# Block writes on SyncE's queue, an earlier split of the receptance, and a second bank for key turns, in a two-layer decoder trunk

## Chip, cores and metric

One core of one Trainium2 chip. The metric is the device time of one launch in microseconds, the median over several runs. Three runs of the kernel before are given, and one execution was taken with the hardware profiler.

## What is computed

Two residual layers over a sequence of 512 tokens of width 2048, all in float32: `x <- x + W_out(mixer(RMSNorm(x)) * silu(gate))`. The first mixer is a gated differential attention with 8 heads (two softmaxes per head on query and key halves of 128, values of 256). The second is a gated RWKV-7 time mixing with 32 heads of width 64. Its core is a scan over tokens:

```python
def step(S, inp):
    r_t, w_t, k_t, v_t, a_t, b_t = inp
    sa = jnp.einsum('bhvk,bhk->bhv', S, a_t)
    S = S * w_t[:, :, None, :] + sa[..., None] * b_t[:, :, None, :] + v_t[..., None] * k_t[:, :, None, :]
    y = jnp.einsum('bhvk,bhk->bhv', S, r_t)
    return S, y
```

with `a = -kk` and `b = kk * a_iclr`, where `kk` is a normalised key. The receptance `r`, key `k`, value `v` and gate are columns of `h @ w_in`, each mixed with its own value one token earlier.

## The kernel before

**Numbers.** Each float32 operand of a large product is split into a rounded part and a rest (`wh` by ScalarE at L105, `wl` by VectorE at L106), and three matmuls take the place of one (`mm3`). So the product of one 128 x 128 weight block with 512 tokens is three matmuls, and TensorE's time is above all in those (L122, L566).

**Order of the work.** Side work (attention of the head before, the scan of the pair before) is cut into steps by Python generators. A `Chain` holds one; `tick` (L169) is called after every matmul of the large products and lets the chain go one step when so many matmuls have passed as the last `yield` said. The framework then orders each engine's instructions; `high_priority(offset=...)` moves an instruction forward by that offset (`AHEAD` 2000, `SCAN` 3000, `SOLVE` 4000), and `issue_after` keeps it behind a given one. Each engine runs its own list in order and waits on semaphores of the others. DMAs are started from the lists of SyncE, ScalarE and GpSimd, each with its own queue.

**First layer** (`layer0`, up to about 955 us). For each head: a product for queries and keys, one for values and gate, and beside them the attention of the head before. `turn_qk` (L291) transposes one of four blocks of 128 tokens of a head's queries and keys on TensorE into a PSUM bank `pt` of tag "pb" (L295), copies it to `qkT` (ScalarE, L298) and subtracts to get the rest `qkL` (VectorE, L299). The tag "pb" has one bank in this pool, shared with the turns of the attention weights (`turn`, L363) and of the result (`turn_y`, L391); the tag "pc" has one, used by `weigh`. For heads 1 to 7 the key blocks 0 and 1 are turned by a chain of their own, and 2 and 3 (the list `rest`) within the attention steps. For head 0 all four are turned by one chain, which `finish` empties after the product of values and gate. At the end of the layer `half_h` and `more_h` transpose the new x and `make_h` (L1088, L1089) scales and splits it into `hH` and `hL` for the second layer's first products (`lora`).

**Second layer** (`layer1`). Two heads make a pair; 16 pairs follow one another, each with four products (k, r, v, gate) of 48 matmuls. For each pair j:

- `stage2` (L1271, L1272) makes `AR`, the scaled receptance and query, and `rf` from the mixed receptance (`mixr`).
- `gram` runs inside the product for v: 16 matmuls `gp` (L1287), copies into `G` (ScalarE, L1294), a sum of squares for the key norms (`ssl`, L1299), and six writes of blocks of G and of the norms to `ltd` in HBM (L1301, L1307).
- `t_solve` loads the blocks from `ltd` into `LT`, spread over 128 partitions (GpSimd's queue, L1341), and inverts unit lower triangular blocks of 32 by 32 on VectorE in 31 steps of two instructions (L1352, L1354), from L1343 to L1355. The result `Tm` is written to `td` (GpSimd's queue, L1356).
- `t_combine`, one pair later, loads `td` into `TT` (SyncE's queue, L1369), transposes on VectorE (`T`, L1378), and makes the off-diagonal blocks with matmuls `px` (L1384, L1394).
- `scan_pair` then goes through 8 chunks: `sm` from VS and G (L1465), copy to `rhs`, `sm` from rhs and TT (L1476), copy to VS, `sm` from VS and BKT (L1483), and VectorE's L1487 (L1490 for the first chunk), which makes the state VS of the next chunk. GpSimd keeps the states (`SA`, L1471) and scales them (`Sg`, L1474), which L1487 reads. GpSimd also masks G (L1316, L1318).
- `stage_v` sums r k over channels (L1206, L1207, on the split `sHx`, `sLx` of `rf`, L1097, L1098), mixes v and makes `y` (L1408). `group_norm` (L1531 to L1537) and `finish_y` work on pair j - 2.

Of the kernel before, what the change touches and what calls it, by code (L numbers as in the profile page):

```python
# [13 lines left out]
F32 = mybir.dt.float32  # L14
# [9 lines left out]
P = 128  # L24
# [263 lines left out]
            w.tile([P, 4, T], F32R, name="qkL", tag="qkL", bufs=1))  # L288


def turn_qk(g, t1s, qkT, qkL, t):  # L291
    nc = g.nc
    pt = g.ps.tile([P, 512], F32, name="pt", tag="pb")
    for c in range(4):
        nc.tensor.transpose(pt[:, c * P : (c + 1) * P], t1s[t][:, c * P : (c + 1) * P], g.ident[:])  # L295
    ts = slice(t * P, (t + 1) * P)
    pv = pt[:].rearrange("p (c q) -> p c q", c=4)
    nc.scalar.copy(qkT[:, :, ts], pv)  # L298
    nc.vector.tensor_sub(qkL[:, :, ts], pv, qkT[:, :, ts].bitcast(F32))  # L299
# [26 lines left out]
def attention(g, h, qkT, qkL, sq, V, VL, G, gap, rows=None, keys=()):  # L326
# [87 lines left out]
    for i in range(NT + 3):  # L414
        if i > 1 and i < NT + 2:
            weigh(i - 2)
        if i > 2:
            turn_y(i - 3)
        if i < NT + 2:
            yield 10  # L420
        while due:
            store(*due.pop())
        if i == NT + 2:
            break
        if 0 < i <= NT:
            turn(i - 1)
        if i < NT:
            scores(i)
        if i == 0 and keys:
            yield 7  # L430
            turn_qk(*keys[0])
            yield 9
            turn_qk(*keys[1])
            yield max(gap - 26, 6)
        else:
            yield gap - 10
    if rows is not None:
        rows += last

# [353 lines left out]
def layer0(g, aps):  # L793
# [3 lines left out]
    with ExitStack() as cx:  # L797
# [91 lines left out]
        for h in range(NH):  # L889
            if h:  # L890
                Chain(g, attention(g, h - 1, *before, 26, keys=rest), 56 if h > 1 else 20)
            t1s = [t1_tile() for _ in range(NT)] if h else t1s
            sq = g.small.tile([P, NT, 2], F32, name="sq", tag="sq")
            qkT = head_qkT(g)

            def keys(n, t1s=t1s, qkT=qkT):
                for t in range(n):
                    turn_qk(g, t1s, *qkT, t)
                    if t < n - 1:
                        yield 20  # L900

            rest = [(g, t1s, *qkT, t) for t in (2, 3)] if h else ()
            if h:
                values = unit_head(g, aps, h, t1s, sq, lambda: Chain(g, keys(2), 6))
            else:
                for ts in ([0, 1], [2, 3]):
                    head_qk(g, t1s, sq, ts)
                Chain(g, keys(NT), 120)
                input_sums(g, pairs, False)
                ps = unit_tok(g, g.hH, g.hL, vg_cols(aps, h), 512)  # L910
                acc1 = g.work.tile([P, 2, 512], F32, name="acc1", tag="acc1", bufs=1)
                G, vg = gates(g)
                vg += [acc1[:, 0], acc1[:, 1]]
                copy_out(g, vg, ps)
                for c in list(g.chains):
                    c.finish(g)
                input_sums(g, pairs, True)
                first_tiles(g, aps, 1)
                values = head_vg(g, h, vg, G)
            before = qkT + (sq,) + values  # L920
            if h == 0:
                Chain(g, rwkv_consts(g, aps))
                g.chains[0].step(g)
# [93 lines left out]
        def half_h(k, half, m, bank=(g.ps, "pa", 2)):  # L1017

            ps = bank[0].tile([P, 512], F32, name="xT", tag=bank[1], bufs=bank[2])
            for i in range(2):  # L1020
                xq, c0 = xs[(k + i) // 4], (k + i) % 4 * P
                for t in range(2):
                    tt, at = 2 * half + t, (2 * i + t) * P
                    if c0 == 0 and half:
                        scale((k + i) // 4, tt)
                    with tc.issue_after(m.ins) if m else ExitStack():
                        nc.tensor.transpose(ps[:, at : at + P], xq[:, tt, c0 : c0 + P], g.ident[:])
            for i in range(2):
                with tc.high_priority(offset=AHEAD):
                    make_h(g, ps[:, 256 * i : 256 * i + 256], KT + k + i, k + i, half)  # L1030

        def begin(m):
# [170 lines left out]
def sum_channels(g, out, ones, x):  # L1203

    h, l = x
    g.nc.tensor.matmul(out, ones, h[:], start=True, stop=False)  # L1206
    g.nc.tensor.matmul(out, ones, l[:], start=False, stop=True)  # L1207
# [68 lines left out]
def gram(g, j, p, before):  # L1276

    nc, w, BK = g.nc, g.work, p.BK
    p.G = w.tile([P, NC_, 2, 2, C], F32, name="G1", tag="G1", bufs=2)
    p.BKT = w.tile([P, NC_, P], F32, name="BKT", tag="BKT", bufs=2)  # L1280
    halves = []
    for c0, tag in ((0, "pb"), (4, "pc")):
        gp = [g.ps.tile([P, 512], F32, name="gp", tag=tag, bufs=2) for _ in range(2)]
        halves.append((c0, gp))
        for i in range(4):
            for h, r_ in ((0, slice(0, C)), (1, slice(C, P))):
                m = nc.tensor.matmul(gp[h][:, i * P : (i + 1) * P], BK[r_, c0 + i, :, :], p.AR[r_, c0 + i, :, :],  # L1287
                                     start=True, stop=True)
    if before:
        with g.tc.issue_after(m.ins):  # L1290
            before.step(g)
    for c0, gp in halves:
        for h in range(2):
            nc.scalar.copy(p.G[:, c0 : c0 + 4, :, h, :], gp[h][:].rearrange("p (u x t) -> p u x t", u=4, x=2))  # L1294
    ps = g.ps.tile([P, 512], F32, name="pt", tag="pb", bufs=2)
    sum_channels(g, ps[:2, :], g.ones[:, 0 : P : C], p.k2)
    ss = w.tile([2, T], F32, name="ssl", tag="thg", bufs=1)
    with g.tc.high_priority(offset=SOLVE if j == D // P - 1 else 0):
        nc.scalar.copy(ss[:], ps[:2, :])  # L1299
        for half in range(2):  # L1300
            nc.scalar.dma_start(  # L1301
                out=g.ltd[j % 2, half, :, :, HALF, :],
                in_=ss[:].rearrange("h (c b t) -> h c b t", c=NC_, b=2)[:, :, half, :])
        for half in range(2):
            for h in range(2):
                q0 = h * C + half * HALF
                nc.scalar.dma_start(  # L1307
                    out=g.ltd[j % 2, half, h, :, 0:HALF].rearrange("c s t -> s c t"),
                    in_=p.G[q0 : q0 + HALF, :, 0, h, half * HALF : (half + 1) * HALF])

# [90 lines left out]
def stage_v(g, j, p, vps):  # L1401
    nc, w = g.nc, g.work
    col = lambda n: g.prm[n][:, j : j + 1]
    ps = g.ps.tile([P, 512], F32, name="pt", tag="pd", bufs=1)
    sum_channels(g, ps[:], g.ones[:], split_act(g, p.rf[:], w, "x"))
    v = shift_mix(g, vps, P, *mus(g, 2, j), "v", 1)
    p.y = w.tile([P, T], F32, name="y", tag="y", bufs=4)
    nc.vector.tensor_mul(p.y[:], ps[:], v[:])  # L1408
# [140 lines left out]
def layer1(g, aps):  # L1549
    nc, tc = g.nc, g.tc  # L1550
    with ExitStack() as cx:
# [22 lines left out]
        for j in range(D // P):  # L1574
# [13 lines left out]
            def behind(m, j=j, p=p):  # L1588
                if j > 1:
                    pairs[j - 2].chain.finish(g)  # L1590
                with tc.issue_after(m.ins):
                    gram(g, j, p, j > 2 and pairs[j - 1].chain)
                if j == 2:
                    pairs[1].chain.wait = 16
                mask_gram(g, p, 0)
# [159 lines left out]
```

## Time and profile before

| what | value |
|---|---|
| median of 3 runs | 2150.44 us (2147.19 to 2150.76) |
| the profiled execution, its own time | 2153.95 us |
| its span in the profile | 2152.2 us |
| TensorE (PE) busy | 2104.0 us, 98% |
| VectorE (DVE) busy | 1613.1 us, 75% |
| ScalarE (ACT) busy | 1153.1 us, 54% |
| GpSimd (POOL) busy | 386.0 us, 18% |
| mean granted clock of TensorE | 0.988 |

The profile shows one execution. An engine's busy time counts its instructions; idle time ahead of an instruction is put down to the instruction whose semaphore came last. In the rows `out<-in` are the program's names of the tiles, `L1384` is a line of the kernel before, and `[0.57 <-DVE T L1378]` says that the engine was idle for 0.57 us until VectorE's T of line 1378 was done. The granted clock is TensorE's share of its full clock. A "frame" in what follows is a pair's own time, counted along with TensorE's matmuls.

### The profile page before, as it was taken

How to read it: one execution, taken by the hardware profiler on the slowest of the kernel's cores; microseconds unless marked ns; L12 is line 12 of the kernel's file. 1: busy time of each engine (PE TensorE's matmuls, PEld its weight loads, DVE VectorE, ACT ScalarE, POOL GpSimd, SP SyncE). 2: the span in 40 equal slices, each digit the busy share in tenths (PEclk: the TensorE clock that was granted, in tenths of full speed). 3: DMA queues.
4: the chain of work that ended last, by engine and by line, in shares of the span. 5: the costliest groups of instructions: out<-in, count | busy, mean ns of one | idle time of the engine just before them, and what ended most of it. 6: DMA issues, size and time to landing. Idle time of an engine off the chain costs nothing.

```text
span 2152.2 us, 34019 instructions
## 1 busy us (share of the span) xinstructions
PE 2104.0 (98%) x11852; PEld 1706.3 (79%) x11852; DVE 1613.1 (75%) x4129; ACT 1153.1 (54%) x2278; POOL 386.0 (18%) x751
## 2 busy tenths in 40 slices
PE   9999999999999999999899999999999999999999
PEld 7788888888887788878677787888888888878887
DVE  6888888888888885667677578777777787767645
ACT  5666556565565543355454455555555556645322
POOL 1011211202113000101322212222222222221001
PEclk9999999999999999999899999999999999999999
DMA  8487978879789836623222223223333233346555
GB/s 264 128 180 188 174 170 187 161 187 175 170 184 221 295 118 186 140 80 104 68 79 68 84 79 94 84 83 94 100 88 92 83 97 91 104 127 191 178 162 120
DMA packets 143101, 294.60 MB, mean 137 GB/s; under 512 B 47968, under 2 KB 65376, under 8 KB 142928
## 3 DMA queue, kind: packets, MB, share of 16 engines
q1 hardware_dynamic: 75072, 178.55, 26.4%
q0 software_dynamic: 25216, 87.74, 22.5%
q10 hardware_dynamic: 42640, 26.14, 4.0%
q8 instruction: 93, 1.52, 0.3%
q14 instruction: 80, 0.66, 0.1%
HBM read 268.71 MB, written 23.66 MB: 136 GB/s over the span
## 4 chain that ended last, share of the span: by engine, by line
PE 36%; DVE 9%; DMA 3%; issue 2%; ACT 1%; POOL 0%; ACTq 0%; SPq 0%; DVEq 0%; POOLq 0%
PE pp L122 22%; PE pt L122 5%; DMA td<-Tm 2%; DVE tmpl L1352 2%; DVE wl L106 2%; DVE Tm L1354 1%; PE gp L1287 1%; PE sm L1465 1%; DMA TT<-td 1%; PE sm L1476 1%; PE sm L1483 1%; PE px L1384 1%; PE px L1394 1%; DVE VS L1487 1%; PE pt L1207 0%
## 5 line engine op out<-in xcount | busy, mean ns | idle before, releaser
L106 DVE TENSOR_TENSOR wl<-wraw,wh 128x1024 fp32r<-128x1024 f32 (+2 forms) x291 | 356.1, 1224 | 222.6 <-ACT wh L105 210.7
L105 ACT CAST wh<-wraw 128x1024 fp32r<-128x1024 f32 (+2 forms) x291 | 304.4, 1046 | 339.3 <-PE pp L122 175.0
L122 PE MATMUL pp<-hH,wl 128*128 128x512 f32 x1024 | 417.0, 407 | 0.0
L122 PE MATMUL pp<-hL,wh 128*128 128x512 f32 x1024 | 415.7, 406 | 0.0
L122 PE MATMUL pp<-hH,wh 128*128 128x512 f32 x1024 | 413.3, 404 | 0.0
L122 PEld LDWEIGHTS pp<-hH,wh 128*128 128x128 f32 x1024 | 195.0, 190 | 35.9 <-issue 1.5
L122 PEld LDWEIGHTS pp<-hL,wh 128*128 128x128 f32 x1024 | 195.0, 190 | 35.6 <-issue 0.3
L122 PEld LDWEIGHTS pp<-hH,wl 128*128 128x128 f32 x1024 | 195.0, 190 | 33.2 <-DVE wl L106 0.5
L566 PE MATMUL pp<-wh,hH 128*128 128x512 f32 x448 | 178.1, 397 | 0.0
L566 PE MATMUL pp<-wh,hL 128*128 128x512 f32 x448 | 176.5, 394 | 0.0
L122 PE MATMUL pp<-wh,hH 128*128 128x512 f32 x372 | 145.8, 392 | 1.7 <-ACT hH L1088 1.6
L122 PE MATMUL pp<-wl,hH 128*128 128x512 f32 x372 | 146.0, 393 | 0.4 <-DVE wl L106 0.4
L122 PE MATMUL pp<-wh,hL 128*128 128x512 f32 x372 | 145.8, 392 | 0.1
L1352 DVE SCALAR_TENSOR_TENSOR tmpl<-LT,Tm 128x60 f32<-128x60 f32 (+24 forms) x496 | 135.0, 272 | 11.6
L1471 POOL COPY SA<-VS 64x64 f32<-64x64 f32 x224 | 63.0, 281 | 442.8 <-DVE VS L1487 348.0
L566 PE MATMUL pp<-wl,hH 128*128 128x512 f32 x448 | 140.6, 393 | 0.1
L1354 DVE TENSOR_TENSOR Tm<-Tm,tmpl 128x60 f32<-128x60 f32 (+24 forms) x496 | 103.6, 209 | 10.5
L566 PEld LDWEIGHTS pp<-wh,hH 128*128 128x128 f32 x448 | 84.7, 189 | 18.1 <-DVE G L527 0.8
L566 PEld LDWEIGHTS pp<-wl,hH 128*128 128x128 f32 x448 | 84.1, 189 | 17.9 <-DVE wl L106 0.5
L566 PEld LDWEIGHTS pp<-wh,hL 128*128 128x128 f32 x448 | 84.8, 189 | 16.4 <-issue 0.2
L1468 ACT COPY rhs<-sm 64x64 f32<-64x64 f32 x256 | 52.9, 207 | 68.4 <-PE sm L1465 65.9
L1478 ACT COPY VS<-sm 64x64 f32<-64x64 f32 x256 | 53.0, 207 | 59.1 <-PE sm L1476 53.8
(394 smaller groups left out, 4494.3 us busy)
## 6 DMA issues: line engine op xcount, KB each, us to landing
wraw<-in_rw_w_in_dram SPq DMA_DIRECT2D x128, 512.0 KB
wraw<-in_da_w_in_dram SPq DMA_DIRECT2D x75, 512.0 KB
wraw<-in_da_w_in_dram POOLq DMA_DIRECT2D x28, 512.0 KB, 6.7
wraw<-in_da_w_out_dram SPq DMA_DIRECT2D x26, 512.0 KB
wraw<-in_rw_w_out_dram SPq DMA_DIRECT2D x26, 512.0 KB
Ta<-in_da_w_in_dram POOLq DMA_DIRECT2D x21, 512.0 KB, 5.8
Tb<-in_da_w_in_dram POOLq DMA_DIRECT2D x21, 512.0 KB, 6.0
Tc<-in_da_w_in_dram POOLq DMA_DIRECT2D x21, 512.0 KB, 5.8
```

The lines of the kernel that those rows point to most:

```text
L105: a = nc.scalar.copy(hi[:, ks], raw[:, ks])
L106: d = nc.vector.tensor_sub(lo[:, ks], raw[:, ks], hi[:, ks].bitcast(F32))
L122: m = nc.tensor.matmul(out, a, b, start=s, stop=e, skip_group_check=skip)
L566: m = nc.tensor.matmul(out[t][:], x, wt[lo][:, k, :], start=first, stop=end and lo == 1 and k == KG - 1, skip_group_check=True)
L1287: m = nc.tensor.matmul(gp[h][:, i * P : (i + 1) * P], BK[r_, c0 + i, :, :], p.AR[r_, c0 + i, :, :], start=True, stop=True)
L1352: nc.vector.scalar_tensor_tensor(tt, LT[:, i : i + 1, i + 1 :].to_broadcast([P, s, n]), n2[:, i : i + 1], Tm[:, 0:s, i : i + 1].to_broadca ...
L1354: nc.vector.tensor_add(Tm[:, 0:s, i + 1 :], Tm[:, 0:s, i + 1 :], tt)
L1384: nc.tensor.matmul(px[hi, c * HALF : (c + 1) * HALF], p.G[lo, c, 0, h, HALF:C], T1[lo, c, :], start=True, stop=True, tile_position=(b0, b0 ...
L1394: nc.tensor.matmul(px[lo, N + c * HALF : N + (c + 1) * HALF], X[hi, c, :], TT[hi, c, h, HALF:C], start=True, stop=True, tile_position=(b0 ...
L1468: nc.scalar.copy(rhs[r_, :], sm[r_, h * C : h * C + C])
L1471: nc.gpsimd.tensor_copy(p.SA[r_, c - 1, :], VS[r_, c, h, :])
L1478: nc.scalar.copy(VS[r_, c, h, :], sm[r_, P : P + C])
```

## The change

The six writes to `ltd` are issued from SyncE's queue instead of ScalarE's. `split_act(p.rf)` is called right after `gram` instead of in `stage_v` (its tiles are those of the key norms' split). In the first layer, key block 3 is turned in bank "pc"; the waits of the chains are changed by two or three matmuls; head 0's blocks 2 and 3 are turned with its attention, like the other heads'; and `make_h` for the first half of the tokens gets the priority `SOLVE`.

```diff
@@ -288,9 +288,9 @@
             w.tile([P, 4, T], F32R, name="qkL", tag="qkL", bufs=1))
 
 
-def turn_qk(g, t1s, qkT, qkL, t):
+def turn_qk(g, t1s, qkT, qkL, t, bank="pb"):
     nc = g.nc
-    pt = g.ps.tile([P, 512], F32, name="pt", tag="pb")
+    pt = g.ps.tile([P, 512], F32, name="pt", tag=bank)
     for c in range(4):
         nc.tensor.transpose(pt[:, c * P : (c + 1) * P], t1s[t][:, c * P : (c + 1) * P], g.ident[:])
     ts = slice(t * P, (t + 1) * P)
@@ -417,7 +417,7 @@
         if i > 2:
             turn_y(i - 3)
         if i < NT + 2:
-            yield 10
+            yield 12
         while due:
             store(*due.pop())
         if i == NT + 2:
@@ -430,10 +430,10 @@
             yield 7
             turn_qk(*keys[0])
             yield 9
-            turn_qk(*keys[1])
-            yield max(gap - 26, 6)
+            turn_qk(*keys[1], "pc")
+            yield max(gap - 28, 6)
         else:
-            yield gap - 10
+            yield gap - 12
     if rows is not None:
         rows += last
 
@@ -899,13 +899,13 @@
                     if t < n - 1:
                         yield 20
 
-            rest = [(g, t1s, *qkT, t) for t in (2, 3)] if h else ()
+            rest = [(g, t1s, *qkT, t) for t in (2, 3)]
             if h:
-                values = unit_head(g, aps, h, t1s, sq, lambda: Chain(g, keys(2), 6))
+                values = unit_head(g, aps, h, t1s, sq, lambda: Chain(g, keys(2), 9))
             else:
                 for ts in ([0, 1], [2, 3]):
                     head_qk(g, t1s, sq, ts)
-                Chain(g, keys(NT), 120)
+                Chain(g, keys(2), 120)
                 input_sums(g, pairs, False)
                 ps = unit_tok(g, g.hH, g.hL, vg_cols(aps, h), 512)
                 acc1 = g.work.tile([P, 2, 512], F32, name="acc1", tag="acc1", bufs=1)
@@ -1026,7 +1026,7 @@
                     with tc.issue_after(m.ins) if m else ExitStack():
                         nc.tensor.transpose(ps[:, at : at + P], xq[:, tt, c0 : c0 + P], g.ident[:])
             for i in range(2):
-                with tc.high_priority(offset=AHEAD):
+                with tc.high_priority(offset=AHEAD if half else SOLVE):
                     make_h(g, ps[:, 256 * i : 256 * i + 256], KT + k + i, k + i, half)
 
         def begin(m):
@@ -1298,13 +1298,13 @@
     with g.tc.high_priority(offset=SOLVE if j == D // P - 1 else 0):
         nc.scalar.copy(ss[:], ps[:2, :])
         for half in range(2):
-            nc.scalar.dma_start(
+            nc.sync.dma_start(
                 out=g.ltd[j % 2, half, :, :, HALF, :],
                 in_=ss[:].rearrange("h (c b t) -> h c b t", c=NC_, b=2)[:, :, half, :])
         for half in range(2):
             for h in range(2):
                 q0 = h * C + half * HALF
-                nc.scalar.dma_start(
+                nc.sync.dma_start(
                     out=g.ltd[j % 2, half, h, :, 0:HALF].rearrange("c s t -> s c t"),
                     in_=p.G[q0 : q0 + HALF, :, 0, h, half * HALF : (half + 1) * HALF])
 
@@ -1402,7 +1402,7 @@
     nc, w = g.nc, g.work
     col = lambda n: g.prm[n][:, j : j + 1]
     ps = g.ps.tile([P, 512], F32, name="pt", tag="pd", bufs=1)
-    sum_channels(g, ps[:], g.ones[:], split_act(g, p.rf[:], w, "x"))
+    sum_channels(g, ps[:], g.ones[:], p.rfs)
     v = shift_mix(g, vps, P, *mus(g, 2, j), "v", 1)
     p.y = w.tile([P, T], F32, name="y", tag="y", bufs=4)
     nc.vector.tensor_mul(p.y[:], ps[:], v[:])
@@ -1590,6 +1590,7 @@
                     pairs[j - 2].chain.finish(g)
                 with tc.issue_after(m.ins):
                     gram(g, j, p, j > 2 and pairs[j - 1].chain)
+                p.rfs = split_act(g, p.rf[:], w, "x")
                 if j == 2:
                     pairs[1].chain.wait = 16
                 mask_gram(g, p, 0)
```

What this does to the order of instructions, at three places. Each fence shows a steady pair, with the rows of one engine in the order in which it runs them. SyncE, before, from the loads of one pair's TT to the next:

```order
149 L1369 DMA TT_9520<-td 32x8x32 x4
150 L78 DMA wraw<-in_rw_w_in_dram 128x1024 x6
151 L1564 DMA upw<-in_rw_decay_up_dram 96x128
152 L1565 DMA upw<-in_rw_iclr_up_dram 96x128
153 L78 DMA wraw<-in_rw_w_in_dram 128x1024 x2
154 L1369 DMA TT_9519<-td 32x8x32 x4
```

and now:

```order
193 L1369 DMA TT_9520<-td 32x8x32 x4
194 L78 DMA wraw<-in_rw_w_in_dram 128x1024
195 L1307 DMA ltd<-G_16193 32x8x32 x3
196 L1301 DMA ltd<-ssl 16x1x32 x2
197 L1307 DMA ltd<-G_16193 32x8x32
198 L78 DMA wraw<-in_rw_w_in_dram 128x1024 x5
199 L1564 DMA upw<-in_rw_decay_up_dram 96x128
200 L1565 DMA upw<-in_rw_iclr_up_dram 96x128
201 L78 DMA wraw<-in_rw_w_in_dram 128x1024 x2
202 L1369 DMA TT_9519<-td 32x8x32 x4
```

The six block writes stand behind the first weight load of a pair and ahead of the other five. (In pairs 0 to 3 they stand elsewhere: the last write of pairs 0 and 1 is behind one more weight load, and of pairs 2 and 3 some stand behind the TT loads of the pair before.)

VectorE, before, ahead of the solve of this pair:

```order
2939 L1129 SCALAR_TENSOR_TENSOR mixv<-pp,mu,mixv 128x511
2940 L1487 SCALAR_TENSOR_TENSOR VS<-sm,gam,Sg 64x64 x2
2941 L71 SCALAR_TENSOR_TENSOR rs_i<-rs_t,rs_i 128x8
2942 L1098 TENSOR_TENSOR sLx<-mixr,sHx 128x512
2943 L68 TENSOR_TENSOR rs_t<-rs_i 128x8
2944 L69 SCALAR_TENSOR_TENSOR rs_t<-rs_t,var 128x8
2945 L71 SCALAR_TENSOR_TENSOR rsg<-rs_t,rs_i 128x8
2946 L1408 TENSOR_TENSOR y<-pt,mixv 128x512
2947 L1537 TENSOR_TENSOR yc<-yc,rsg 128x512
2948 L106 TENSOR_TENSOR wl<-wraw,wh 128x1024
2949 L1487 SCALAR_TENSOR_TENSOR VS<-sm,gam,Sg 64x64 x2
2950 L1343 TENSOR_SCALAR LT<-LT 128x32
```

and now:

```order
2944 L69 SCALAR_TENSOR_TENSOR rs_t<-rs_t,var 128x8
2945 L71 SCALAR_TENSOR_TENSOR rsg<-rs_t,rs_i 128x8
2946 L1537 TENSOR_TENSOR yc<-yc,rsg 128x512
2947 L106 TENSOR_TENSOR wl<-wraw,wh 128x1024
2948 L1129 SCALAR_TENSOR_TENSOR mixv<-pp,mu,mixv 128x511
2949 L1408 TENSOR_TENSOR y<-pt,mixv 128x512
2950 L1487 SCALAR_TENSOR_TENSOR VS<-sm,gam,Sg 64x64 x2
2951 L1343 TENSOR_SCALAR LT<-LT 128x32
```

The solve (L1343) stood behind the second VS pair of the scan and now stands behind the first; that first pair stood ahead of the last steps of the root, y and yc, and now stands behind them; sLx has moved further up, ahead of the first weights of V.

TensorE, before, at the same pair's px and gp, and behind it now:

```order
5431 L122 MATMUL pp<-hH,wl 128x512
5432 L1384 MATMUL px<-T_15452,G_14815 32x32 x8
5433 L1287 MATMUL gp<-AR,BK 128x128 x4
5434 L1384 MATMUL px<-T_15452,G_14815 32x32 x8
5435 L1287 MATMUL gp<-AR,BK 128x128 x12
5436 L1394 MATMUL px<-TT_9519,X 32x32 x16
```

```order
5429 L122 MATMUL pp<-hH,wl 128x512
5430 L1384 MATMUL px<-T_15452,G_14815 32x32 x16
5431 L1287 MATMUL gp<-AR,BK 128x128 x16
5432 L1394 MATMUL px<-TT_9519,X 32x32 x16
```

All 16 px now stand ahead of all 16 gp. On VectorE, AR stood ahead of both transposes T of the pair and now stands behind them. On GpSimd, the load of LT stood behind the scaling Sg of the first chunk's state and now stands ahead of it, with both masks (L1316, L1318) right behind. And on TensorE the sums L1206 and L1207 of `stage_v` stand right behind the last matmul of the product for v, where 11 to 16 matmuls of the next product stood ahead of them.

## The prediction

> **What bounds the kernel now.** I read the page's engine table first, then TensorE's waits, then the timelines of the places where it waits.
>
> ```profile
> PE 2104.0 (98%) x11852; PEld 1706.3 (79%) x11852; DVE 1613.1 (75%) x4129; ACT 1153.1 (54%) x2278; POOL 386.0 (18%) x751
> ```
>
> TensorE is busy for 98% of 2152.2 us, and the change takes no matmul away. So it can gain only from TensorE's idle 48 us, and from stretches in which its clock is low. TensorE's waits (columns: microseconds in total, times, longest):
>
> ```profile
> PE px L1384 <- DVE T L1378: 14.0, 16, 3.5
> PE px L1384 <- DVE y L1408: 5.4, 1, 5.4
> PE pt L295 <- DVE qkL L299: 5.3, 7, 1.0
> PE pt L295 <- ACT t L280: 4.3, 3, 3.4
> PE lora L122 <- ACT hH L1088: 1.3, 1, 1.3
> PE pt L363 <- DVE yTl L400: 1.0, 1, 1.0
> PE sm L1465 <- DVE VS L1487: 0.9, 3, 0.5
> ```
>
> The largest is the wait for T, the transposed inverse of the second layer, once a pair. The change aims at that row and at the two L295 rows. The long ones among these waits are paid twice, as four windows behind them and one of a steady pair show (columns: stretch, length, busy time of PE, PEld, DVE, ACT and POOL, granted clock, DMA share, GB/s):
>
> ```profile
> 1152.00:1164.00 12.00, 12.00 (x84) 9.18 (x82) 5.26 (x19) 4.23 (x12) 1.18 (x3) 0.57 0.28 86
> 1211.00:1222.00 11.00, 10.90 (x93) 9.09 (x94) 1.58 (x4) 5.85 (x11) 1.78 (x2) 0.53 0.18 52
> 1279.00:1287.00 8.00, 8.00 (x76) 6.63 (x75) 0.00 (x0) 5.29 (x11) 1.78 (x2) 0.57 0.15 49
> 1344.00:1349.00 5.00, 5.00 (x76) 4.52 (x75) 0.00 (x0) 3.78 (x9) 0.14 (x1) 0.66 0.24 79
> 1466.00:1528.00 62.00, 61.05 (x422) 49.72 (x420) 47.66 (x131) 34.76 (x78) 15.52 (x36) 1.00 0.32 91
> ```
>
> At a clock of 0.57, 12 us of TensorE time hold 6.8 us of work. The four windows lose 5.2, 5.2, 3.4 and 1.7 us. From about 1405 us on every pair looks like the last row, at full clock. The waits ahead of these windows, and of two steady pairs, in TensorE's timeline (start, length; in brackets the idle time ahead and its releaser):
>
> ```profile
> 1151.62 0.69 PE L1384 MATMUL px<-T,G 32*32 32x32 f32 x16 [3.51 <-DVE T L1378]
> 1208.86 0.69 PE L1384 MATMUL px<-T,G 32*32 32x32 f32 x16 [1.00 <-DVE T L1378]
> 1211.10 0.95 PE L1384 MATMUL px<-T,G 32*32 32x32 f32 x16 [1.55 <-DVE T L1378]
> 1277.57 0.69 PE L1384 MATMUL px<-T,G 32*32 32x32 f32 x16 [0.62 <-DVE T L1378]
> 1342.71 0.69 PE L1384 MATMUL px<-T,G 32*32 32x32 f32 x16 [1.56 <-DVE T L1378]
> 1466.96 0.69 PE L1384 MATMUL px<-T,G 32*32 32x32 f32 x16 [0.57 <-DVE T L1378]
> 1528.28 0.69 PE L1384 MATMUL px<-T,G 32*32 32x32 f32 x16 [0.54 <-DVE T L1378]
> ```
>
> The first five rows are pairs 2, 3 (two waits), 4 and 5; together 8.2 us. The other 11 waits of the 14.0 us share 5.8 us, 0.53 each.
>
> **First layer: key turns.** Six heads wait 0.7 to 1.0 us for a bank that the third key block's subtraction still reads; the seventh of the L299 waits, 0.7 us, lies in head 0. The fourth block's own bank takes these six away: 5.3 - 0.7 = **-4.6**. Nothing else uses bank "pc" until the first weighing, 22 ticks on. The wait ahead of the first key turn goes from 6 to 9 matmuls. Two neighbours in TensorE's timeline give the spacing:
>
> ```profile
> 447.21 0.39 PE L566 MATMUL pp<-wh,hH 128*128 128x512 f32 x1
> 447.43 0.39 PE L566 MATMUL pp<-wh,hL 128*128 128x512 f32 x1
> ```
>
> At 0.22 to 0.23 us, three are worth 0.7, more than either of the two short waits that make 4.3 - 3.4 = 0.9: **-0.9**. The two ticks more before turning y are worth 0.45 of the 1.0 us at L363: **-0.4**. In the input of the second layer the order puts one square sum behind the copy that TensorE awaits instead of ahead of it: of 1.3 us I take **-0.9**, half of it to all of it.
>
> Head 0 is different. TensorE, then ScalarE:
>
> ```profile
> 104.00 0.79 PE L566 MATMUL pp<-wh,hH 128*128 128x512 f32 x1
> ```
> ```profile
> 103.39 0.56 ACT L248 COPY acc<-pp 128x512 f32<-128x512 f32 x1
> ```
>
> Key blocks 2 and 3 leave this place, and their 0.7 + 3.4 us of waits with them. But the next matmul, L566 at 104.00, stands right at the end (103.95) of the copy at L248 that empties a bank for it. In the new order that copy comes about 0.4 us sooner, so most of the wait changes its name and stays: **-0.5** (0 to -4). Sum of the first layer: **-7.3**.
>
> **Second layer: when T is ready.** Pair 8 in the steady state, one chain: the copies of G, the last block write on ScalarE's queue, the load on GpSimd's, VectorE's order ahead of the solve, its end, T, and TensorE's need for VS.
>
> ```profile
> 1470.35 2.06 ACT L1294 COPY G<-gp 128x512 f32<-128x512 f32 x4
> ...
> 1477.89 0.31 ACTq L1307 DMA_DIRECT2D ltd<-G  x1
> ```
> ```profile
> 1481.49 2.05 POOL L1341 DMA_DIRECT2D LT<-ltd  x4 [2.63 <-issue]
> ```
> ```profile
> 1481.39 1.23 DVE L106 TENSOR_TENSOR wl<-wraw,wh 128x1024 fp32r<-128x1024 f32 x1
> 1482.65 0.75 DVE L1129 SCALAR_TENSOR_TENSOR mixv<-pp,mu,mixv 128x511 f32<-128x511 f32 x1
> 1483.31 0.59 DVE L1487 SCALAR_TENSOR_TENSOR VS<-sm,gam,Sg 64x64 f32<-64x64 f32 x2
> ...
> 1486.26 1.47 DVE L1537 TENSOR_TENSOR yc<-yc,rsg 128x512 f32<-128x512 f32 x1
> ...
> 1489.88 0.60 DVE L1487 SCALAR_TENSOR_TENSOR VS<-sm,gam,Sg 64x64 f32<-64x64 f32 x2
> 1490.51 0.18 DVE L1343 TENSOR_SCALAR LT<-LT 128x32 f32<-128x32 f32 x1
> ```
> ```profile
> 1522.18 0.41 DVE L1355 TENSOR_TENSOR Tm<-Tm,LT 128x256 f32<-128x256 f32 x1
> ```
> ```profile
> 1527.79 0.44 DVE L1378 STREAM_TRANSPOSE T<-TT 64x256 f32<-64x256 f32 x1 [0.61 <-DMA TT<-td]
> ```
> ```profile
> 1486.02 0.38 PE L1465 MATMUL sm<-VS,G 128*128 128x128 f32 x2
> ```
>
> The copies of G end at 1472.4, yet the last of the six writes is issued 5.5 us later, since on ScalarE's queue they stand between casts and copies that wait for TensorE. On SyncE's queue nothing stands between them but the copy of the norms; at 0.3 to 0.6 us an issue they are out by about 1475.8, and the loads follow 2.1 us sooner, at 1479.4. (The next weight load stood on SyncE's queue until about 1476 anyhow, so nothing behind them is late.) But the loads did not bind: VectorE came to L1343 only at 1490.5, right behind the second VS pair. What counts is the new place of the solve, behind the first VS pair and ahead of wl and the second. By the durations above that is about 1485.3, so it starts 5.2 us sooner; wl and a VS pair now fall inside it (1.8 us), and at its end another wl stands ahead of the last steps (0.8 net). T comes **2.6 us** sooner.
>
> Is that enough? The px need 0.54. After the change all gp stand behind all px, and AR is made behind the second transpose: mixr and AR put it some 3.3 us behind the first transpose's start, 1528.5, where TensorE, not stalled, reaches gp at 1529.05. So 2.0 us sooner is enough, and the 11 waits go: **-5.8**.
>
> The price is on the first VS pair, which now stands behind yc, wl, mixv and y. From the point where wl began (1481.39, the root not yet done), with 0.6 for the rest of the root, 1.3 for yc, then 1.3, 0.7 and 0.6 for wl, mixv and y and the pair's own 0.6, it ends at 1486.5; less the 0.57 us that this pair no longer loses at its own px, at 1485.9. TensorE wants it at 1486.02 - 0.57 = 1485.45, if it has not waited there. From below, there is no stall (the L1465 row above shows 0.5 at most); from above, 1.5 us, if yc stays at 1.47 and GpSimd's masks, now right behind the load, slow two of the operations by 0.4 each. The sum says 0.4, the row 0.0 to 0.5; I take 0.2, between them, over 11 pairs: **+2.2**. The moved sums (L1206, L1207) cost nothing new: their operands are made before the weights of V are split.
>
> For pairs 4 and 5 the same 2.6 us cover the 0.62, and of the 1.56 all but 0.5 (gp needs 1.5 more than px): **-1.7**; pair 4's low clock goes with its wait (-3.4), pair 5's I leave.
>
> Pairs 2 and 3 wait for more than the solve. The write of pair 2's solution and that of a steady pair, in the views of DMA issues (last column: issue to landing):
>
> ```profile
> td<-Tm POOLq DMA_DIRECT2D x1, 128.0 KB, 5.1
> ```
> ```profile
> td<-Tm POOLq DMA_DIRECT2D x1, 128.0 KB, 2.8
> ```
>
> 2.3 us of pair 2's 3.51 come from a weight load beside it that the change leaves there. In the order of instructions these two solves move by a step or two only: **-1.5** for both (0 to -4), with their low clocks left in place. Pairs 0 and 1 I leave as they are (their writes now stand behind one weight load each; 0 to +2).
>
> [...]
>
> **Sum.** -7.3 - 5.8 + 2.2 - 1.7 - 3.4 - 1.5 = -17.5 against the profiled execution's 2153.95 (1.75 more than its span): **2136.5 us**. That execution stands 3.5 above the median of the three runs shown, so the median would fall by 14, 0.65%.
>
> **Rivals.**
> [...]
> - *A wait of the same size takes T's place* (TensorE at gp for AR, or for the second transpose): the second layer gives nothing, the first its 7.3: 2146.6. For it: VectorE is 75% busy, and AR has moved behind both transposes.
> - *Slower: the first VS pair is late in every steady pair.* If the masks and yc collide as in the upper bound, each of 11 pairs stalls 1.5 at L1465 and saves 0.53: +10.7, and one more low clock of 3.4; with the first layer's -7.3 that is +6.8: 2160.7. It decides from a stall of 1.2 us on (11 x 0.67 = 7.4). The same place stalls if the load's wait on GpSimd, with Sg now queued behind it, lasts past 1483 instead of 1479.4.
> - *The key turns gain nothing* (the pb wait returns at the next turn): 2142; counted within the range.
>
> **Chances.** Forecast 0.42, the better clocks 0.15, the same-size wait 0.22, slower 0.21. A measurement of this kernel tells about 0.2%, 4.3 us, from no change, so against 2150.4 the middle is 2146.1 to 2154.7. The third case lies astride that edge and splits evenly, with a little more of it and of the slower case in the middle: faster 0.64, same 0.17, slower 0.19. The range of 8 in 10 reaches from 2121 to 2157; the forecast's own, by its bounds, from 2128 to 2145.
>
> **What would show it.** In the changed profile: the L295 wait for qkL down to under 1 us; an L566 wait of 3 us at about 103; the T wait at L1384 under 6 us in all, with pairs 2 and 3 left; L1343 at about 19 us behind the start of px instead of 23.5; the L1465 wait for VS between 0 and 3 us. I am wrong if L1465 or L1287 shows 6 us or more, or if L1343 does not start sooner.

## The result: no change that can be told

| | median us | lowest to highest | runs |
|---|---|---|---|
| before | 2151.53 | 2147.19 to 2165.05 | 12 |
| changed | 2155.06 | 2144.86 to 2158.59 | 12 |

The ratio of changed to before is 0.9998, with a 95% interval of 0.9978 to 1.0019 (it goes by the means, 2153.28 and 2153.67 us; by the medians the changed kernel is 0.16% slower). The forecast was 2136.5 us, 0.65% faster. The profiled execution of the changed kernel took 2153.4 us, with a span of 2151.7, where before had 2153.95 and 2152.2. The changed kernel's line numbers are those of before up to L1592.

TensorE's waits in the changed kernel (total, times, longest):

```profile
PE gp L1287 <- DVE AR L1271: 9.8, 12, 0.8
PE px L1384 <- DVE T L1378: 5.3, 9, 1.0
PE pp L566 <- ACT acc L248: 4.9, 1, 4.9
PE px L1384 <- DVE y L1408: 3.8, 1, 3.8
...
PE pt L363 <- DVE yTl L400: 1.1, 1, 1.1
...
PE pt L295 <- ACT t L280: 0.7, 1, 0.7
```

The wait for T has gone from 14.0 to 5.3 us, and a wait for AR of 9.8 us has come, 0.82 in each of 11 steady pairs (the twelfth, 0.76 in pair 1, was there before with 0.6): 15.1 in place of 14.6 (14.0, and 0.6 for AR). The L295 waits for qkL are gone, and head 0's waits bear the name L566 now. The L1465 wait for VS is not in the list any more.

The clock has moved in the same way. Stretches of the changed kernel (busy time of PE, PEld, DVE, ACT and POOL, then the granted clock, DMA share and GB/s):

```profile
1153.00:1164.00 11.00, 10.73 (x56) 8.15 (x55) 5.42 (x17) 5.20 (x15) 4.48 (x9) 1.00 0.14 48
1211.00:1222.00 11.00, 11.00 (x56) 8.94 (x56) 9.18 (x27) 5.79 (x14) 6.40 (x11) 1.00 0.40 126
1391.20:1398.00 6.80, 6.80 (x57) 5.46 (x54) 0.69 (x1) 4.55 (x9) 1.78 (x2) 0.50 0.10 19
1582.30:1589.10 6.80, 6.80 (x63) 5.70 (x60) 0.69 (x1) 4.07 (x8) 1.78 (x2) 0.50 0.12 27
```

Pairs 2 and 3 keep the full clock, which they had not. In exchange the half clock comes behind pairs that had none. By the trace's own clock records, before had four stretches at half clock between 1100 and 1900 us (10.2, 10.2, 6.8, 3.4), 30.7 us that lose 15.3; the changed kernel has seven (3.4, 6.8, 3.4, 6.8, 3.4, 6.8, 3.4), 34.1 us that lose 17.1.

Over the whole span, TensorE's waits of 0.25 us and more have hardly changed: 17.0 us before and 15.9 now up to 955 us, 21.3 and 20.8 behind that. Nor has what half clock costs, 27.8 and 28.0 us.

So the gain was made and given back. The first gp of pair 4 stood at 1212.7 us and stands at 1199.2, that of pair 6 at 1343.3 and 1326.7: 16.6 us ahead. Pair 8 is 12.3 ahead, pair 11 5.4, pair 14 2.0, and pair 15 2.0 behind. Nine steady pairs lose 2.1 us each.

One steady pair shows how. First SyncE and GpSimd in the kernel before:

```profile
1517.13 3.21 SPq L78 DMA_DIRECT2D wraw<-in_rw_w_in_dram  x2
1526.01 1.82 SPq L1369 DMA_DIRECT2D TT<-td  x4
```
```profile
1523.15 1.00 POOL L1356 DMA_DIRECT2D td<-Tm  x1 [3.08 <-DVE s L1520]
```

Now the same in the changed kernel, then its VectorE:

```profile
1505.82 2.33 SPq L78 DMA_DIRECT2D wraw<-in_rw_w_in_dram  x2
1513.45 1.82 SPq L1369 DMA_DIRECT2D TT<-td  x4
```
```profile
1508.87 0.99 POOL L1356 DMA_DIRECT2D td<-Tm  x1 [4.84 <-DVE Tm L1355]
```
```profile
1472.91 0.59 DVE L1487 SCALAR_TENSOR_TENSOR VS<-sm,gam,Sg 64x64 f32<-64x64 f32 x2
1473.53 0.18 DVE L1343 TENSOR_SCALAR LT<-LT 128x32 f32<-128x32 f32 x1
```
```profile
1506.56 1.22 DVE L106 TENSOR_TENSOR wl<-wraw,wh 128x1024 fp32r<-128x1024 f32 x1
1507.69 0.17 DVE L1354 TENSOR_TENSOR Tm<-Tm,tmpl 128x8 f32<-128x8 f32 x1
1507.89 0.42 DVE L1355 TENSOR_TENSOR Tm<-Tm,LT 128x256 f32<-128x256 f32 x1
...
1515.27 0.44 DVE L1378 STREAM_TRANSPOSE T<-TT 64x256 f32<-64x256 f32 x1 [4.40 <-DMA TT<-td]
1515.63 1.18 DVE L106 TENSOR_TENSOR wl<-wraw,wh 128x1024 fp32r<-128x1024 f32 x1
1516.84 0.44 DVE L1378 STREAM_TRANSPOSE T<-TT 64x256 f32<-64x256 f32 x1
1517.32 0.75 DVE L1129 SCALAR_TENSOR_TENSOR mixr<-pp,mu,mixr 128x511 f32<-128x511 f32 x1
1518.10 0.69 DVE L1271 TENSOR_TENSOR AR<-mixr,E 128x512 f32<-128x512 f32 x1
```

TensorE in the same place:

```profile
1516.43 0.69 PE L1384 MATMUL px<-T,G 32*32 32x32 f32 x16
1517.34 0.69 PE L1384 MATMUL px<-T,G 32*32 32x32 f32 x16 [0.22 <-DVE T L1378]
1518.85 2.06 PE L1287 MATMUL gp<-AR,BK 64*128 64x128 f32 x32 [0.82 <-DVE AR L1271]
```

The solve does start right behind the first VS pair. To compare the two kernels, count back from the moment at which TensorE is ready for its next px: 1527.74 before (the row at 1528.28 less its wait of 0.54), 1516.43 now. Tm is ready 8.1 us ahead of that moment instead of 5.1, so 3.0 us sooner, and its write is issued 7.6 us ahead instead of 4.6. But the first transpose T starts only 1.2 us sooner, 1.16 us ahead instead of 0.05 behind.

The two weight loads of 512 KB have hardly moved: the first is issued 10.6 us ahead of px in both kernels, the second 7.7 us ahead before and 8.6 now. Before, the write followed the second by 3.2 us; now it follows by 1.1 and lands 4.5 us behind its issue, where 2.8 were shown before. T is then just in time or late by 0.2 us, AR comes another 1.5 us behind the second transpose, and TensorE stands for 0.82 us ahead of gp. (Counted from this pair's first gp at 1455.3, T seems to start no sooner, at 60.0 us against 60.2. That count holds 1.7 us lost at half clock right behind that gp.)

In the view of DMA issues around that write (issue to landing in the last column):

```profile
td<-Tm POOLq DMA_DIRECT2D x1, 128.0 KB, 4.5
```

### The profile page after: what moved, and what is told of

Its sections match the earlier page's. It is cut to its first block, busy times and chain, and to the rows that moved or that the text cites. A ratio compares the mean times of both kernels' runs of the same rounds, so it can differ in the third digit from the quotient of the medians.

```text
span 2151.7 us, 34077 instructions
## 1 busy us (share of the span) xinstructions
PE 2105.0 (98%) x11852; PEld 1708.5 (79%) x11852; DVE 1612.5 (75%) x4129; ACT 1154.1 (54%) x2278; POOL 389.8 (18%) x751
## 4 chain that ended last, share of the span: by engine, by line
PE 71%; DVE 15%; DMA 7%; ACT 3%; issue 3%; POOL 0%; ACTq 0%; SPq 0%; POOLq 0%; DVEq 0%
PE pp L122 31%; PE pp L566 20%; PE pt L122 5%; DVE wl L106 4%; DMA td<-Tm 3%; PE gp L1287 2%; DMA TT<-td 1%; DVE tmpl L1352 1%; PE sm L1465 1%; PE sm L1483 1%; PE sc L122 1%; PE o L122 1%; PE sm L1476 1%; ACT wh L105 1%; PE lora L122 1%
## 5 line engine op out<-in xcount | busy, mean ns | idle before, releaser
L566 PE MATMUL pp<-wh,hH 128*128 128x512 f32 x448 | 178.4, 398 | 5.0 <-ACT acc L248 4.9
L566 PE MATMUL pp<-wh,hL 128*128 128x512 f32 x448 | 176.9, 395 | 0.0
L566 PE MATMUL pp<-wl,hH 128*128 128x512 f32 x448 | 141.5, 394 | 0.4 <-DVE wl L106 0.4
L1471 POOL COPY SA<-VS 64x64 f32<-64x64 f32 x224 | 55.8, 249 | 469.4 <-DVE VS L1487 361.2
L566 PEld LDWEIGHTS pp<-wh,hH 128*128 128x128 f32 x448 | 85.0, 190 | 23.1 <-ACT acc L248 5.3
L566 PEld LDWEIGHTS pp<-wl,hH 128*128 128x128 f32 x448 | 85.0, 190 | 18.1 <-DVE wl L106 0.8
L566 PEld LDWEIGHTS pp<-wh,hL 128*128 128x128 f32 x448 | 85.0, 190 | 16.6
```

Source lines behind the costliest of these rows:

```text
L566: m = nc.tensor.matmul(out[t][:], x, wt[lo][:, k, :], start=first, stop=end and lo == 1 and k == KG - 1, skip_group_check=True)
L1471: nc.gpsimd.tensor_copy(p.SA[r_, c - 1, :], VS[r_, c, h, :])
```

## The experiments

**The parts alone.** The first theory was that the second layer's block writes make both the gain at the early pairs and the loss behind, through AR's place and the late landing; the rival was that the early split does it. Three kernels, each the kernel before with some of the edits.

*First layer alone* (`l0_only`):

```diff
...
-            turn_qk(*keys[1])
+            turn_qk(*keys[1], "pc")
...
-                values = unit_head(g, aps, h, t1s, sq, lambda: Chain(g, keys(2), 6))
+                values = unit_head(g, aps, h, t1s, sq, lambda: Chain(g, keys(2), 9))
...
-                Chain(g, keys(NT), 120)
+                Chain(g, keys(2), 120)
...
-                with tc.high_priority(offset=AHEAD):
+                with tc.high_priority(offset=AHEAD if half else SOLVE):
```

> The kernel before with the first layer's edits alone (second bank, ticks, head 0's blocks, priority of make_h). Theory (the second layer gives back what it gains, the first layer gains what its bank waits cost): the six bank waits go (4.6 us), head 0 loses 0.9, so 2 to 6 us faster than before; the second layer's T waits stay 14 us with their low clocks at pairs 2 to 5. Rival (the first layer gains nothing since the waits return at the end of it): within 1 us of before, with as much idle TensorE time up to 955 us as before.

Measured: 2149.39 us against 2152.86, ratio 0.9981 (0.9965 to 0.9997): 4 us faster, between 0.6 and 7.5, as the theory had it. The L1384 wait for T is 14.2 us, as before. Its low clocks at pairs 2 and 3 were shorter in the profiled execution, the fastest of the 12 (3.4 and 6.8 us, against 10.2 and 10.2 and two more), though the second layer is the same program, so the clock's stretches alone differ by some 10 us from one execution to another.

*Block writes alone* (`ltd_only`):

```diff
-            nc.scalar.dma_start(
+            nc.sync.dma_start(
                 out=g.ltd[j % 2, half, :, :, HALF, :],
...
-                nc.scalar.dma_start(
+                nc.sync.dma_start(
                     out=g.ltd[j % 2, half, h, :, 0:HALF].rearrange("c s t -> s c t"),
```

> The kernel before with the six block writes on SyncE's queue and nothing else. Theory (this one edit moves the solve ahead, which brings a weight load beside the write of the solution and puts AR behind both transposes): TensorE's waits at L1287 for AR of about 10 us over 12 pairs, low clocks behind several steady pairs and none at pairs 2 to 4, time within 6 us of before. Rival (the early split of the receptance does it): no AR wait at L1287, steady pairs as before, 5 to 15 us faster than before.

Measured: 2157.98 us, ratio 1.0021 (1.0007 to 1.0035). Its waits:

```profile
PE gp L1287 <- DVE AR L1271: 9.5, 12, 0.8
PE pt L295 <- DVE qkL L299: 5.2, 7, 1.0
PE px L1384 <- DVE T L1378: 4.4, 7, 0.9
```

The theory holds: the whole trade, T's wait for AR's, comes with this one edit, and pairs 2 to 4 keep the full clock. Of the low clocks behind steady pairs only two stretches (10.2 and 3.4 us) show, in the fastest of the 12 executions, which is the one profiled.

*Early split alone* (`rfs_only`):

```diff
-    sum_channels(g, ps[:], g.ones[:], split_act(g, p.rf[:], w, "x"))
+    sum_channels(g, ps[:], g.ones[:], p.rfs)
...
                     gram(g, j, p, j > 2 and pairs[j - 1].chain)
+                p.rfs = split_act(g, p.rf[:], w, "x")
```

> The kernel before with the receptance split right behind the gram products and nothing else. Theory: AR stays ahead of the transposes in the order, so no AR wait; low clocks of pairs 2 to 5 stay; within 6 us of before. Rival (this edit makes the loss): AR waits of 5 us or more at L1287, and 5 us or more slower than before.

Measured: 2196.84 us, ratio 1.0208 (1.0194 to 1.0223). The theory fails. The rival's two figures are met, AR waits of 8.3 us and a loss of 45 us, but AR is the smaller part: T waits are 30.3 us, and half clock costs 48.1 us of the span instead of 27.8. ScalarE's timeline has the reason for T:

```profile
1473.46 2.06 ACT L1294 COPY G<-gp 128x512 f32<-128x512 f32 x4 [4.34 <-PE gp L1287]
1475.38 0.66 ACT L1097 CAST sHx<-mixr 128x512 fp32r<-128x512 f32 x1
...
1491.51 0.31 ACTq L1307 DMA_DIRECT2D ltd<-G  x1
```

With the cast moved ahead, all but the first of the six writes stand behind or among copies that wait for px on ScalarE's queue, and the last goes out 16 us behind the copies of G, not 5.5. LT is loaded from 1495.0 on, and L1343 starts at 1499.6, 24.1 us behind those copies instead of 18.1. The two edits of the second layer are not independent: the split can stand early only if the writes are off this queue.

**The place of AR.** In the changed kernel, T's transposes have the priority of the scan and AR has none, and the order puts both transposes first. `ar_first` holds the transposes behind AR:

```diff
-    nc.vector.tensor_mul(p.AR[:, :, 1, :], r[:].rearrange("p (c t) -> p c t", c=NC_), p.E[:, :, 1:])
+    g.ar = nc.vector.tensor_mul(p.AR[:, :, 1, :], r[:].rearrange("p (c t) -> p c t", c=NC_), p.E[:, :, 1:]).ins
...
-        with g.tc.issue_after(g.centred) if g.centred else ExitStack():
+        with g.tc.issue_after(g.centred) if g.centred else ExitStack(), g.tc.issue_after(g.ar):
             nc.vector.transpose(T1[r_], TT[r_, :, h, 0:HALF])
...
             p = pairs[j]
+            stage2(g, j, r, p)
             if j:
...
-            stage2(g, j, r, p)
```

> The changed kernel with one constraint more: the transposes T of a pair stand behind the making of AR on VectorE, and AR's place in the program is ahead of the loads of TT. Theory (AR behind the transposes is what costs, 0.82 us a pair at L1287 and the low clock behind it): the AR wait of 9.8 us goes to under 2, the low clocks of the steady pairs (34 us at half) go, and the time falls by 15 to 25 us, to about 2130 to 2140. Rival (T itself is late, since its write meets weight loads): the wait moves to L1384 for T at the same size, low clocks stay, time within 4 us of the changed kernel.

Measured: 2128.68 us (2127.6 to 2129.07), ratio 0.9888 to before (0.9873 to 0.9902). That is 24 us faster than before, and 1.1% faster than the changed kernel too (0.9888 against its 0.9998), a little past the far end of what the theory expected. The rival falls: the write of the solution still lands late (3.3 to 4.5 us in the steady pairs), and with AR made first that does not matter. VectorE and TensorE at the same place:

```profile
1501.38 1.22 DVE L106 TENSOR_TENSOR wl<-wraw,wh 128x1024 fp32r<-128x1024 f32 x1 [2.44 <-ACT wh L105]
1502.52 0.74 DVE L1129 SCALAR_TENSOR_TENSOR mixr<-pp,mu,mixr 128x511 f32<-128x511 f32 x1
1503.30 0.69 DVE L1271 TENSOR_TENSOR AR<-mixr,E 128x512 f32<-128x512 f32 x1
1503.91 0.90 DVE L1378 STREAM_TRANSPOSE T<-TT 64x256 f32<-64x256 f32 x2
```
```profile
1504.49 0.69 PE L1384 MATMUL px<-T,G 32*32 32x32 f32 x16
1505.11 0.48 PE L1287 MATMUL gp<-AR,BK 64*128 64x128 f32 x2
1505.53 0.69 PE L1384 MATMUL px<-T,G 32*32 32x32 f32 x16
1506.14 2.05 PE L1287 MATMUL gp<-AR,BK 64*128 64x128 f32 x30
```

AR is made in VectorE's idle time ahead of TT's landing, and TensorE goes through px and gp without a gap. A steady pair now has the full clock, and 61.77 of 62 us are busy:

```profile
1444.00:1506.00 62.00, 61.77 (x437) 50.56 (x438) 47.35 (x131) 35.37 (x79) 16.31 (x36) 1.00 0.31 95
```

The rest is the clock. Against the changed kernel, gaps of 0.25 us and more in the second layer fall from 20.8 to 8.7 us, and what half clock costs over the whole span from 28.0 to 10.9: together 29 us, of a span that is 25.8 shorter.

**The landing of the write.** `hold_load` is the changed kernel (its lines two further on from L81) with the two weight loads held behind the TT loads on SyncE's queue:

```diff
-    with g.tc.issue_after(g.last) if g.last and not queue else ExitStack():
+    with g.tc.issue_after(g.last) if g.last and not queue else ExitStack(), \
+            g.tc.issue_after(g.hold) if g.hold else ExitStack():
...
+    g.hold = None
...
-            nc.sync.dma_start(
+            g.tt = nc.sync.dma_start(
...
+            g.hold = g.tt.ins if j > 2 else None
             u = g.wraw.tile([RK, 2, P], F32, name="upw", tag="wraw")
```

> The changed kernel, with the two weight loads that stood ahead of a pair's TT loads on SyncE's queue put behind them; AR stays behind both transposes. Theory (the write of the solution takes 3.4 to 4.5 us instead of 2.3 since 512 KB weight loads run beside it, which eats most of the 2 us that the solve gains): the write lands in 2.3 to 2.6 us, T is 1 to 2 us sooner, the 12 AR waits of 0.82 fall to under 3 us in all and the low clocks of the steady pairs mostly go; 10 to 25 us faster than the changed kernel. Rival (the place of AR alone decides, T's time does not): the AR waits stay at about 0.8 each, and the time within 4 us of the changed kernel.

Measured: 2142.37 us, ratio 0.9944 (0.9924 to 0.9965). The theory holds. The write of a steady pair lands sooner, the AR waits are down to 4, and the steady low clocks are gone:

```profile
td<-Tm POOLq DMA_DIRECT2D x1, 128.0 KB, 2.8
```
```profile
PE px L1386 <- DVE T L1380: 7.7, 3, 6.9
...
PE gp L1289 <- DVE AR L1273: 2.7, 4, 0.8
```

So the landing is a cause of its own. By the packets, 11 of the 13 writes with no weight packet beside them ended 2.3 to 2.5 us behind their issue (the others 2.9 and 3.2); in the changed kernel the 11 writes of pairs 4 to 14, with 128 to 171 weight packets beside them, took 3.4 to 5.6. T of a steady pair (4 to 13) now starts 1.7 to 3.0 us ahead of the moment at which TensorE is ready for px. Where it is 2.6 us or more ahead, TensorE reaches gp 1.0 us behind its first px and does not wait.

The one wait of 6.9 us is at pair 2 (1148 us), and 17.1 us of half clock lie around it, so 6.9 + 8.5 us are lost there. It is probably a price of the hold itself: three weight loads go out at 1085.6 us, behind the TT loads, where three had gone between 1065.0 and 1077.1 in the changed kernel. TensorE waits 2.5 us for the rounded part of one at 1092.3 (6.8 us of half clock follow), and L1343 of pair 2 stands 36.2 us behind its gp instead of 26.2. So the 12 us by which this kernel beats the one before may understate what the landing costs.

`ar_ltd` is the kernel before with the writes' edit and AR's, `ar_l1` has the early split too, `ar_before` is the kernel before with AR's edit alone.

> The kernel before with the block writes on SyncE's queue and AR held ahead of the transposes; receptance split and first layer as before. Theory (these two carry the whole gain of the second layer): 2129 to 2138 us, no AR wait, T waits under 4 us. Rival (the early split of the receptance is needed for the gain): T or AR waits of 6 us or more, and 2142 us or more.

> As the last one, with the receptance split early as well (so the second layer of the changed kernel with AR held ahead of the transposes, first layer as before). Theory (the early split changes nothing once the writes are on SyncE's queue): within 3 us of the last one, and 2 to 8 us slower than the changed kernel with AR first, by the first layer's share. Rival (the early split costs): over 4 us slower than the last one.

> The kernel before with AR held ahead of the transposes and nothing else. Its steady order is that of the kernel before. Theory (the constraint by itself gives nothing, T is still late): T waits of 12 us or more, low clocks at pairs 2 to 5, within 5 us of before. Rival (the constraint is a gain of its own): 10 us or more faster than before.

| kernel | median us | ratio to before |
|---|---|---|
| `ar_ltd` | 2140.76 | 0.9931 (0.9914 to 0.9949) |
| `ar_l1` | 2132.86 | 0.9898 (0.9880 to 0.9916) |
| `ar_before` | 2143.26 | 0.9943 (0.9926 to 0.9960) |

`ar_ltd` lies between the two expectations, with T waits of 2.0 us and no AR wait but pair 1's: the place of AR and the writes are most of it. `ar_l1` is 8 us faster than that, which no theory had expected; of the 11.4 us by which the spans of these two profiles differ, 4.4 are half clock, 1.2 gaps in the second layer, and 1.9 gaps in the first, which is the same program in both. What makes the rest was not tried. `ar_before` gained 12 us, which is what the rival had: the constraint is a gain of its own. So with AR first in both kernels, the change of this document is worth about as much again (0.9888 against 0.9943). Its steady order is that of before, its T waits are 11.2 us, and it has three low stretches behind 1100 us instead of four (10.2, 6.8 and 6.8 us). How far its 12 us come from the early pairs' order and how far from where the low stretches fall stays open.

**The first layer's terms**, on the fastest kernel, whose runs spread least (2127.7 to 2129.9 us). `ar_again` is `ar_first` once more, `ar_nobank` takes key block 3 back to bank "pb" (`turn_qk(*keys[1])`), and `ar_nohead0` takes head 0's turns back (`rest` empty for head 0, `keys(NT)`).

> The changed kernel with AR held ahead of the transposes, once more, to stand beside the next two on one chip: 2127 to 2131 us, 0.98 to 0.99 of before.

> The same with the fourth key block back in bank pb. Theory (the bank is worth its six or seven waits and nothing more): 4 to 6 us slower than the one beside it, and the L295 waits for qkL back at 4.6 to 5.3 us. Rival (the waits come back elsewhere, so the bank is worth nothing): within 1.5 us of it.

> The same with all four key blocks of head 0 turned ahead of head 1, as before. Theory (TensorE waits at that place for the copy of the accumulators anyway, and the wait only changes its name): within 1.5 us of the one with head 0's blocks moved; L295 waits of 3 to 4 us in place of the 4.9 at L566. Rival (the move is worth the 4.1 us of waits that it took away): 3 to 5 us slower.

| kernel | median us | ratio to before |
|---|---|---|
| `ar_again` | 2128.61 | 0.9896 (0.9882 to 0.9910) |
| `ar_nobank` | 2130.46 | 0.9904 (0.9890 to 0.9918) |
| `ar_nohead0` | 2128.30 | 0.9899 (0.9883 to 0.9914) |

`ar_nobank` is 1.9 us slower by the medians, and the intervals overlap. No L295 wait for qkL has come back, so the theory of the bank falls; the time lies between the two expectations. VectorE's and TensorE's timelines at head 2's turns say why, first before, then in `ar_nobank`:

```profile
303.81 1.23 DVE L106 TENSOR_TENSOR wl<-Td,wh 128x1024 fp32r<-128x1024 f32 x1
304.95 0.68 DVE L299 TENSOR_TENSOR qkL<-pt,qkT 128x512 fp32r<-128x512 f32 x1
```
```profile
302.02 0.60 PE L295 MATMUL pt<-ident,t 128*128 128x128 f32 x4
305.69 0.66 PE L295 MATMUL pt<-ident,t 128*128 128x128 f32 x4 [1.00 <-DVE qkL L299]
```
```profile
304.87 1.23 DVE L106 TENSOR_TENSOR wl<-Td,wh 128x1024 fp32r<-128x1024 f32 x1 [1.09 <-ACT wh L105]
...
306.09 0.67 DVE L299 TENSOR_TENSOR qkL<-pt,qkT 128x512 fp32r<-128x512 f32 x1
```
```profile
304.29 0.60 PE L295 MATMUL pt<-ident,t 128*128 128x128 f32 x4
306.81 0.66 PE L295 MATMUL pt<-ident,t 128*128 128x128 f32 x4
```

In both, the subtraction stands behind a split of weights. But counted from the third block's own turn (302.02 and 304.29), that split starts 1.8 us later in the one and 0.6 us later in the other, and the subtraction ends at 3.6 and at 2.5 us; the fourth block's turn, 2.5 to 2.7 us behind the third if it need not wait, waits in the one only. What has moved the turn against the split are probably the chains' tick counts, since the other edits of the first layer lie at head 0 and at its end; they were not tried alone. With them in place the bank is at most a spare.

`ar_nohead0` is as fast as `ar_again`, with head 0's waits under their old name (L295 for t 4.2 us in all, none at L566 of 4.9). That bears out the prediction's reading that the wait only changes its name.

## Why the prediction was wrong

- **T 2.6 us sooner: the step that failed.** The solve starts where it was said to: L1343 stands 19.2 to 19.6 us behind the start of px in pairs 9, 11 and 13, which have no half clock in them (19 was said). Tm is ready 3.0 us sooner, a little better than said. The prediction then carried this through to T as if the way from Tm to T stayed as long. In pairs 6 to 13 it got 1.4 to 2.2 us longer, so T starts only 0.7 to 1.7 us sooner: the write came forward into two weight loads that hardly moved. The prediction had both facts in hand, the two loads ahead of TT in SyncE's order and the price of a load beside the write (5.1 us against 2.8 at pair 2). It did not ask what would be under way at the write's new time. `hold_load` shows that this is the cause: with the loads out of the way the write lands in 2.3 to 2.5 us and the steady low clocks go.
- **2.0 us are enough for gp: too few.** AR comes 3.5 us behind the first transpose's start, not 3.3, since a split of weights stands between the transposes, and TensorE without a wait reaches gp 1.0 us behind its first px. By that T had to start about 2.6 us sooner, all that was forecast, with nothing to spare. (The recorded 1528.5 for the first transpose is in no row; from 1527.79, the row shown, the sum does give 2.0.) With 0.7 to 1.7 us, gp waits for AR at 0.82 a pair. That is the rival of a wait of the same size in T's place, with its place and its engine; it was given 0.22. It is also the prediction's own sign of being wrong: L1287 shows 9.8 us, where 6 were named.
- **The first VS pair: 0.2 us a pair were too much.** TensorE does not wait there in the changed kernel (no L1465 row); yc took 0.69 to 0.76 us in the steady pairs, not 1.3 (before, 1.46 to 1.47 in the eight pairs in which it ran 0.93 us beside GpSimd's mask L1318, 0.68 to 0.69 in the six with no mask beside it). Beside the masks' new place wl took 1.67 us in nine pairs, not 1.22; mixv (0.75) and y (0.69) took no longer there than without a mask. The slower rival did not come.
- **Pairs 2 to 5:** 1.5 and 1.7 us of waits and one low clock were said; by pair 4 the changed kernel was 13.5 us ahead, by pair 6 16.6. Pair 2's wait fell from 3.51 to 1.04, as its write no longer met a weight load (landing 2.3 us), and the low clocks of pairs 2 and 3 went, which the chances have as the better clocks (0.15). "A weight load that the change leaves there" was wrong in this pair: the block writes now hold the load back on SyncE's queue, until 1142.1, 1.2 us behind the write.
- **What the steady pairs would do to the clock was left out.** Each wait was priced by its length. The half clock behind seven pairs cost 17 us more, as much as the early pairs had gained. By the two profiles it is this, more than the length of the waits (which fell by 1.6 us in all), that brought the sum to zero.
- **The first layer's 7.3 us:** 4 by the kernel with that part alone (0.6 to 7.5); by TensorE's waits up to 955 us it is 2.8 there, and 1.1 in the changed kernel's profile. The six waits (4.6 us) went, but probably by the ticks and not by the bank. At head 0 the mechanism was right and the size was not: 4.9 us at L566 in place of 4.1 at L295, 0.9 more where 0.5 less was said. The wait at L363 stayed (1.0 and 1.1), one of the two short L295 waits stayed (0.7), and the waits for hH and hL at the second layer's input fell by 0.4, not 0.9. The last head's attention waits 2.0 us more in the changed kernel's profile (a second 0.70 at L566, and 0.4 at each of three places), which was not foreseen.

No wait of a steady pair in the changed kernel is over 1.0 us, and yet in seven pairs 0.8 to 2.7 us of them, with small px and gp matmuls between, have a stretch of half clock at or right behind the first gp.

## What to carry to other kernels

When a transfer moves forward, list what else is under way at its new time: here the write of the solution went out 3.0 us sooner, met two loads that had hardly moved, and lost 1.4 to 2.2 us of that. When a wait goes, list everything that the waiting engine needs in the next microseconds, and look in the new order where each is made; the cheapest fix here was one constraint that put AR into VectorE's idle time, and it was worth 1.1% where the whole change had been worth nothing (and 0.6% on the kernel before). And a gap in TensorE that recurs may cost more than its length (in the changed kernel 0.8 to 2.7 us of waits in each of seven pairs came with 17.1 us lost at half clock), so a last half microsecond a pair can be worth removing.

## What the runs showed of the hardware

- In the profiles of before and of the changed kernel TensorE's half clock (0.50) came in stretches of 3.4, 6.8, 10.2 or 13.7 us, but for the one at the end of each span. The seven in the second layer of the changed kernel behind its steady pairs start at 1326.3, 1391.2, 1456.0, 1582.3, 1708.6, 1834.9 and 1899.8 us, that is 19, 19, 37, 37, 37 and 19 times 3.413 us apart, and 3.413 us is the shortest of the stretches recorded between the ends. Of the 11 steady pairs with an AR wait there, the five that lost 1.1 us or more in waits all had such a stretch, and of the six that lost 0.8 to 1.0 only two. What decides it for those six was not shown.
- The 128 KB writes of td from GpSimd's queue ended 2.3 to 2.5 us behind their issue in `hold_load` with no weight load beside them (11 of 13 writes), and 3.4 to 5.6 us behind it in the changed kernel's pairs 4 to 14, with one or two loads of 512 KB from SyncE's queue beside them.
